# A float32 decoder trunk on one core: position parts ahead of their DMA copies, a fixed order of first loads, and PSUM banks emptied in two rounds

## The chip, the cores and the metric

The kernel runs on 1 core of one Trainium2 chip. The metric is the device time of one execution in microseconds (us); of several runs the median is taken. A stretch of time is given as start:end in us from the start of the span, the time from the first to the last instruction of the profiled execution.

## The reference, cut to what matters

Two layers of a decoder trunk, 512 tokens by 1024 columns, float32 throughout:

```python
def hybrid_layer(x, ...):
    h = rms_norm(x, g_pre)
    proj = h @ w_in                      # 1024 -> 3628 columns, split into four groups of 4 heads x 64
    o_a = dilated_mixture_attention(rope(a_q), rope(a_k), a_v)
    o_b = mla_attention(b_cq, b_ckv, b_kr, ...)       # low-rank q and kv, one rotary key
    o_c = nsa_attention(rope(c_q), ...)               # compressed, selected and window keys
    o_d = stick_breaking_attention(d_q, d_k, d_v)
    mixed = concat(o_a * silu(a_g), o_b * silu(b_g), o_c * silu(c_g), o_d * silu(d_g))
    return x + rms_norm(mixed @ w_out, g_post)
```

For branch C, `compress_blocks` takes 31 overlapping blocks of 32 tokens of a key (and of a value), adds a position embedding to each, and sends each block, flattened to 2048, through two small matrices. The position embedding is what "position parts" means below.

## The kernel before, in words

**Numbers in two parts.** Products are made as three matmuls of two-part numbers: a first part (the value rounded to fp32r) and a remainder (value minus first part). Wherever a result leaves a PSUM bank to be a matmul operand again, ScalarE (ACT) copies the first part out of the bank, and VectorE (DVE) subtracts it from the bank and writes the remainder. Weights come from HBM by DMA into one of four raw buffers; ACT, DVE or GpSimd (POOL) casts the first part, and POOL subtracts (L310, L320).

**The start** (`run`). The x rows (four blocks of 128), the gain `g_pre`, the first part of the constants (with the identity that transposes need) and the first weight chunks are loaded by DMAs from SyncE's queue (SP). TensorE (PE) meanwhile runs WARM matmuls of ones by ones, whose result nobody reads. `norm_t` takes one block of x: square with a sum on ACT (L415), logarithm and exponential on ACT (L397, L398), product with the gain on DVE in two halves (L419), four PE transposes per half into one bank (L424), first part on ACT (L431), remainder on DVE (L432). The first projection matmuls (L456, L457, L459) read 256 columns, so blocks 0 and 1 both, at once. Banks 77 and 78 are the two halves of block 0, banks 79 and 80 those of block 1.

**The projections** (`chunk`, `proj_b`, `proj_d`, `value_out`, `gate`) fill banks on PE; `d_query`, `evac96`, `value_out` and the value part of `proj_b` empty a bank in two pieces: first part of piece 0, remainder of piece 0, first part of piece 1, remainder of piece 1. `block_parts` makes the stationary operands of the block compression: for each of two slots it issues 4 (keys) or 2 (values) DMA copies from SBUF to SBUF that write columns 0 to 495, and then writes the position parts into columns 496 to 511, with a small copy on ACT (L878) and a small subtraction on DVE (L879), both 128x8. PE reads the slots at L905.

**Attention** runs beside the projections: `turn` transposes probabilities (L1105) and empties the bank (L1108 on ACT, L1109 on DVE), `pv` multiplies with the values (L1121), `stick` is branch D with its scans and sums on DVE (L1045 to L1059), `softmax` the others (L1019, L1021, L1029).

**What sets the order.** The program is written by generators that mix attention with projections, and then class `Order` reorders it: it gives each instruction a cost and a latency, builds the graph of what must follow what (`graph`), and simulates the five engines forward and backward, several times. In this graph a bank is one cell: each access to it follows the latest access by every engine, two reads included. A DMA into a slot counts as covering everything between its first and last element. `keep` then fixes the found order on each engine. Engines, and the SP queue, work strictly in that order, so an instruction that waits holds up all that stands behind it on its engine.

Of the kernel before, what the change touches and what calls it, by code (L numbers as in the profile page):

```python
# [172 lines left out]
START = (0, 'c', 1, 'g', 'w', 'w', 'w', 2, 3, 'w')  # L173
PRE = 2
WARM = 32
# [9 lines left out]
class Build:  # L185
# [224 lines left out]
    def norm_t(self, b, x, gpre, h=None):  # L410

        nc = self.nc
        h = h or self.F.get(2)
        ss = self.col()
        nc.scalar.activation(h.ap, x.ap, AF.Square, accum_out=ss)  # L415
        r = self.rstd(ss, D)
        for half in range(2):
            q = slice(512 * half, 512 * half + 512)
            nc.vector.scalar_tensor_tensor(h[:, q], x[:, q], r, gpre[:, q], op0=OP.mult, op1=OP.mult)  # L419
        for half in range(2):  # L420
            t = self.ps(*self.wide)
            for k in range(4):
                kk = half * 4 + k
                nc.tensor.transpose(t[:, k * 128:k * 128 + 128], h[:, kk * 128:kk * 128 + 128], self.ident)  # L424
            tv = t.rearrange("p (k c) -> p k c", k=4)
            pair = [self.nh[j][2 * half:2 * half + 2] for j in range(2)]
            n = 4 if all(q.i == p.i + 2 for p, q in pair) else 2
            for q in range(4 // n):
                hi, lo = (self.R.ap[:, p[q].i * 512:(p[q].i + n) * 512].rearrange("p (k c) -> p k c", k=n)[
                    :, :, b * 128:b * 128 + 128] for p in pair)  # L430
                nc.scalar.copy(hi, tv[:, n * q:n * q + n])  # L431
                nc.vector.tensor_tensor(lo, tv[:, n * q:n * q + n], hi.bitcast(F32), OP.subtract)  # L432
            self.psfree(t)
        h.free()
# [45 lines left out]
    def value_out(self, outs):  # L480

        vs = [self.R.get(2) for _ in range(2)]
        with self.soon():
            for p, out in enumerate(outs):
                ov = out.rearrange("p (b h c) -> p b h c", b=2, h=4)
                for j, v in enumerate(vs):
                    self.value_parts(v.ap.rearrange("p (e b t c) -> p t b e c", e=2, b=4, t=2)[:, :, 2 * p:2 * p + 2],
                                     ov[:, :, 2 * j:2 * j + 2])
                self.psfree(out)
        return vs  # L490
# [87 lines left out]
    def values(self, out):  # L578
# [3 lines left out]
        with self.soon():  # L582
            nc.scalar.copy(v.ap, out)
            self.psfree(out)
            t = self.ps(*self.wide)
            for b in range(NB):
                nc.tensor.transpose(t[:, b * 128:b * 128 + 128], v[:, b * 128:b * 128 + 128], self.ident)
            d = self.R.get(2)
            self.value_parts(d.ap.rearrange("p (e b t c) -> p t b e c", e=2, b=4, t=2),
                             t.rearrange("p (b e c) -> p b e c", b=4, e=2))  # L590
            self.psfree(t)
# [3 lines left out]
    def value_parts(self, d, src):  # L595
        self.nc.scalar.copy(d[:, 0], src)
        self.nc.vector.tensor_tensor(d[:, 1], src, d[:, 0].bitcast(F32), OP.subtract)
# [39 lines left out]
    def proj_b(self, l):  # L637
# [110 lines left out]
        for p in range(2):  # L748
# [4 lines left out]
            with self.soon():  # L753
                ov = out.rearrange("p (b h c) -> p b h c", b=2, h=4)
                for j in range(2):
                    dv = V[j].ap.rearrange("p (h b t c) -> p t b h c", h=2, b=4, t=2)
                    self.value_parts(dv[:, :, 2 * p:2 * p + 2], ov[:, :, 2 * j:2 * j + 2])
# [13 lines left out]
    def evac96(self, out, d):  # L771
        nc = self.nc
        with self.soon():
            for j in range(2):
                s = out[64 * j:64 * j + 64]
                nc.scalar.copy(d[j][0:64, 0], s)
                nc.vector.tensor_tensor(d[j][0:64, 1], s, d[j][0:64, 0].bitcast(F32), OP.subtract)  # L777
        self.psfree(out)

    def d_query(self, p, out):  # L780
        nc = self.nc
        with self.soon():
            for j in range(2):
                s, x = self.R.get(), out[64 * j:64 * j + 64]
                nc.scalar.copy(s[0:64], x)
                nc.vector.tensor_tensor(s[64:128], x, s[0:64].bitcast(F32), OP.subtract)
                self.Dq[2 * p + j] = s
# [77 lines left out]
    def block_parts(self, parts, n, pos):  # L865
# [5 lines left out]
        for i in range(2):  # L871
            d = self.R.get(2)
            for j, s in enumerate(parts):
# [3 lines left out]
            p, q = self.small[:, pos + 8 * i:pos + 8 * i + 8], d.v(2)[:, :, 496:512:2]  # L877
            nc.scalar.copy(q[:, 0], p)  # L878
            nc.vector.tensor_tensor(q[:, 1], p, q[:, 0].bitcast(F32), OP.subtract)  # L879
# [522 lines left out]
    def run(self):  # L1402
# [3 lines left out]
        self.setup()  # L1406
        for step in START:
# [6 lines left out]
            else:  # L1414
                nc.sync.dma_start(xs[step].ap, self.aps["x"][128 * step:128 * step + 128])
        nc.sync.dma_start(self.c[:, C_MA:], c[:, C_MA:])
# [86 lines left out]
class Order:  # L1503
# [6 lines left out]
    def __init__(self, nc, tc):  # L1510
        self.tc = tc
# [95 lines left out]
    def graph(self):  # L1607
# [3 lines left out]
        for k, i in enumerate(self.ins):  # L1611
# [23 lines left out]
            self.after.append(sorted(d))  # L1635
        self.then = [[] for _ in self.ins]
# [22 lines left out]
    def backward(self):  # L1659
# [11 lines left out]
        for _ in range(n):  # L1671
# [7 lines left out]
            for j in self.after[k]:  # L1679
                f = self.eng[j]  # L1680
                busy, lat, _, extra = self.cost[j]
                if f == e == 0:
# [12 lines left out]
    def forward(self, rank):  # L1695
# [13 lines left out]
        for _ in self.ins:  # L1709
# [23 lines left out]
            for j in self.then[k]:  # L1733
                f = self.eng[j]
                ready[j] = max(ready[j], free[e] if f == e == 0 else end[k] + (self.SEES[f] if f != e or e == 4 else 0))
# [16 lines left out]
def build(nc, tc, aps):  # L1752
    with tc.tile_pool(name="sb", bufs=1) as sb, \
# [4 lines left out]
        o = Order(nc, tc)  # L1758
# [46 lines left out]
```

## Time and profile before

| | us |
|---|---|
| median of 3 runs | 662.58 (661.51 to 663.36) |
| the profiled execution | 661.76 |
| its span | 660.0 |
| PE busy in it | 633.2 |
| ACT, DVE, POOL busy | 471.4, 455.5, 384.9 |

The profiled execution took 1.76 us beyond its span and stands 0.82 us under the median. Its page gives the busy time of each engine; the trace gives each instruction's start and duration, and what ended the idle time before it. PE matmuls overlap, so a busy PE is not a PE at its peak. A DVE or POOL instruction's duration includes time in which it has been started but waits for a port of the memory.

### The profile page before, as it was taken

Reading aid. Unit: us, or ns where it says so; the run is one execution under the profiler, and the core shown is the slowest. Engines: PE = TensorE matmul, PEld = TensorE weight load, DVE = VectorE, ACT = ScalarE, POOL = GpSimd, SP = SyncE. Lnnn points to the kernel's source line nnn. Section 1 sums busy time; section 2 is a strip of 40 time slices with the busy share of each in tenths; the row PEclk is TensorE's granted clock in tenths of the full one; section 3 lists DMA queues with packets and bytes.
Section 4 is the critical chain, followed back from the end, with each engine's and each line's share of the span. In section 5 each row is a group of like instructions: output and inputs, shape, how many; then the busy total and the mean of one; then the engine's idle time right before and its main releaser. Section 6 shows DMA issues by size and latency. Waiting matters only on the chain.

```text
span 660.0 us, 10416 instructions
## 1 busy us (share of the span) xinstructions
PE 633.2 (96%) x3488; PEld 531.5 (81%) x3488; DVE 455.5 (69%) x964; ACT 471.4 (71%) x1053; POOL 384.9 (58%) x301
## 2 busy tenths in 40 slices
PE   8999998699999999999999999999999999999996
PEld 8988876588768789877889878877887778987885
DVE  4837999975788666459594875976557956756623
ACT  6276767396989878997434765867987896779911
POOL 3482658467974772986373335195695845666620
PEclk9999999799999999999999999999999999999998
DMA  9465222853453246644444232028546422562121
GB/s 327 153 210 166 77 64 51 202 145 95 124 162 129 65 125 163 189 159 131 141 138 125 81 97 75 1 51 221 159 136 164 149 94 64 137 184 65 65 96 64
DMA packets 36487, 83.25 MB, mean 126 GB/s; under 512 B 7185, under 2 KB 17809, under 8 KB 36433
## 3 DMA queue, kind: packets, MB, share of 16 engines
q1 hardware_dynamic: 36432, 82.59, 42.5%
q8 instruction: 27, 0.44, 0.3%
q14 instruction: 28, 0.22, 0.1%
HBM read 57.66 MB, written 4.19 MB: 94 GB/s over the span
## 4 chain that ended last, share of the span: by engine, by line
PE 65%; ACT 12%; DVE 11%; POOL 3%; issue 3%; DMA 3%; SPq 1%; DVEq 0%; ACTq 0%; POOLq 0%
PE bank L456 9%; PE bank L457 9%; PE bank L459 8%; PE bank L446 6%; PE bank L447 6%; PE bank L448 6%; PE bank L1121 6%; PE bank L1105 5%; ACT arena_f L1021 3%; ACT arena_f L1029 3%; PE bank L974 2%; PE bank L975 2%; DVE arena_f L1057 2%; DVE arena_f L1059 2%; PE bank L905 2%
## 5 line engine op out<-in xcount | busy, mean ns | idle before, releaser
L320 POOL TENSOR_TENSOR arena_r<-raw,arena_r 128x512 fp32r<-128x512 f32 (+1 forms) x150 | 201.6, 1365 | 131.7 <-ACT arena_r L315 91.3
L456 PE MATMUL bank<-arena_r 128*128 128x512 f32 (+1 forms) x416 | 158.9, 387 | 1.0 <-DVE arena_f L725 0.4
L457 PE MATMUL bank<-arena_r 128*128 128x512 f32 (+1 forms) x416 | 157.8, 384 | 0.0
L459 PE MATMUL bank<-arena_r 128*128 128x512 f32 (+1 forms) x416 | 107.4, 380 | 1.1 <-POOL arena_r L320 1.0
L446 PE MATMUL bank<-arena_r 128*128 128x256 f32 (+1 forms) x280 | 96.2, 346 | 0.2 <-DVE arena_r L777 0.2
L1121 PE MATMUL bank<-arena_r 128*128 128x256 f32 (+4 forms) x368 | 85.6, 321 | 10.6 <-DVE arena_r L1109 8.0
L447 PE MATMUL bank<-arena_r 128*128 128x256 f32 (+1 forms) x280 | 95.7, 343 | 0.0
L448 PE MATMUL bank<-arena_r 128*128 128x256 f32 (+1 forms) x280 | 95.0, 342 | 0.0
L1109 DVE TENSOR_TENSOR arena_r<-bank,arena_r 128x512 fp32r<-128x512 f32 (+2 forms) x122 | 71.8, 597 | 29.7 <-ACT arena_r L1108 27.4
L456 PEld LDWEIGHTS bank<-arena_r 128*128 128x128 f32 x416 | 79.8, 192 | 14.2 <-DVE arena_f L725 1.0
L457 PEld LDWEIGHTS bank<-arena_r 128*128 128x128 f32 x416 | 79.7, 192 | 12.1 <-DVE arena_r L432 0.2
L459 PEld LDWEIGHTS bank<-arena_r 128*128 128x128 f32 x416 | 74.2, 189 | 15.6 <-POOL arena_r L320 2.1
L1105 PE MATMUL bank<-consts,arena_f 128*128 128x128 f32 x408 | 79.3, 276 | 1.5 <-DVE arena_r L1109 0.7
L1021 ACT ACTIVATE arena_f<-arena_f,stats 128x512 f32<-128x512 f32 (+3 forms) x128 | 71.1, 557 | 12.3 <-DVE stats L1019 11.6
L1019 DVE CUSTOM_DVE_ANT_0 arena_f<-bank,consts 128x128 f32<-128x128 f32 (+3 forms) x128 | 59.4, 483 | 25.3 <-PE bank L975 14.7
L1121 PEld LDWEIGHTS bank<-arena_r 128*128 128x128 f32 (+1 forms) x368 | 52.8, 163 | 23.7 <-DVE arena_r L1109 9.7
L1108 ACT CAST arena_r<-bank 128x512 fp32r<-128x512 f32 (+2 forms) x122 | 61.5, 512 | 12.9 <-PE bank L1105 10.1
L1029 ACT ACTIVATE arena_f<-arena_f,stats 128x512 f32<-128x512 f32 (+3 forms) x128 | 66.7, 557 | 2.6 <-DVE stats L1028 2.2
L1105 PEld LDWEIGHTS bank<-consts,arena_f 128*128 128x128 f32 x408 | 53.0, 141 | 16.1 <-DVE arena_r L1109 2.5
L315 ACT CAST arena_r<-raw 128x1024 fp32r<-128x1024 f32 (+2 forms) x55 | 56.1, 1024 | 13.1 <-PE bank L457 4.1
L446 PEld LDWEIGHTS bank<-arena_r 128*128 128x128 f32 x280 | 53.1, 190 | 6.7 <-DVE arena_r L777 0.7
L310 POOL TENSOR_TENSOR arena_r<-raw,arena_r 128x512 fp32r<-128x512 f32 x34 | 47.0, 1393 | 18.7 <-ACT arena_r L309 13.3
(159 smaller groups left out, 1175.4 us busy)
## 6 DMA issues: line engine op xcount, KB each, us to landing
raw<-w_in SPq DMA_DIRECT2D x56, 512.0 KB, 3.8
raw<-w_out SPq DMA_DIRECT2D x16, 512.0 KB, 3.4
arena_r<-arena_r SPq DMA_DIRECT2D x56, 128.0 KB, 2.4
arena_r<-arena_r SPq DMA_DIRECT2D x80, 64.0 KB, 2.0
arena_f<-x SPq DMA_DIRECT2D x8, 512.0 KB, 4.1
raw<-w1k SPq DMA_DIRECT2D x8, 512.0 KB, 4.3
raw<-w1v SPq DMA_DIRECT2D x8, 512.0 KB, 3.7
arena_r<-arena_r SPq DMA_DIRECT2D x8, 256.0 KB, 3.2
```

The source lines that it names most:

```text
L320: nc.gpsimd.tensor_tensor(lo[:, q], raw[:, q], h[:, q].bitcast(F32), OP.subtract)
L446: mm(out, wh, xh, start=start, stop=False, skip_group_check=True)
L447: mm(out, wh, xl, start=False, stop=False, skip_group_check=True)
L448: mm(out, wl, xh, start=False, stop=stop, skip_group_check=True)
L456: mm(out[:, q], wh[:, k, :], self.h(0, k)[:, q], start=k == 0, stop=False, skip_group_check=True)
L457: mm(out[:, q], wh[:, k, :], self.h(1, k)[:, q], start=False, stop=False, skip_group_check=True)
L459: mm(out[:, q], wl[:, k - 8, :], self.h(0, k - 8)[:, q], start=False, stop=k == 15, skip_group_check=True)
L1021: nc.scalar.activation(x, x, AF.Exp, bias=nm[:, j:j + 1], scale=-1.0, accum_out=l[:, j:j + 1])
L1029: nc.scalar.activation(parts[j], parts[j], AF.Copy, scale=rj)
L1105: nc.tensor.transpose(t[:, 128 * j:128 * j + 128], b, self.ident)
L1109: nc.vector.tensor_tensor(lo[:, :w], t[:, :w], hi[:, :w].bitcast(F32), OP.subtract)
L1121: mm(o, v, x, start=first and n == 0, stop=last and n == 2 * len(jobs) - 1, skip_group_check=True)
```

## The change

Three edits, and 8 more warm-up matmuls:

- `both` (new) copies the first parts of all pieces of a bank on ACT, and then subtracts all remainders on DVE. `norm_t`, `value_out`, `values`, `evac96`, `d_query` and the value part of `proj_b` go through it (L431 and L432, L596 and L597, L776 and L777, L785 and L786 before; L597 and L599 after).
- `block_parts` writes the position parts of a slot before it issues the slot's DMA copies (L878 and L879 before; L870 and L871 after).
- START, the order of the first loads, becomes x0, gain, constants, x1, two weights, x2, x3, two weights; `Order` now gets the names of these loads and has an edge from each to the next, so that they keep this order on the SP queue. WARM goes from 32 to 40.

```diff
-START = (0, 'c', 1, 'g', 'w', 'w', 'w', 2, 3, 'w')
+START = (0, 'g', 'c', 1, 'w', 'w', 2, 3, 'w', 'w')
-WARM = 32
+WARM = 40
...
-            for j in range(2):
-                s = out[64 * j:64 * j + 64]
-                nc.scalar.copy(d[j][0:64, 0], s)
-                nc.vector.tensor_tensor(d[j][0:64, 1], s, d[j][0:64, 0].bitcast(F32), OP.subtract)
+            self.both([(x[0:64, 0], x[0:64, 1], out[64 * j:64 * j + 64]) for j, x in enumerate(d)])
...
+    def both(self, parts):
+        for hi, _, src in parts:
+            self.nc.scalar.copy(hi, src)
+        for hi, lo, src in parts:
+            self.nc.vector.tensor_tensor(lo, src, hi.bitcast(F32), OP.subtract)
...
             d = self.R.get(2)
+            p, q = self.small[:, pos + 8 * i:pos + 8 * i + 8], d.v(2)[:, :, 496:512:2]
+            nc.scalar.copy(q[:, 0], p)
+            nc.vector.tensor_tensor(q[:, 1], p, q[:, 0].bitcast(F32), OP.subtract)
             for j, s in enumerate(parts):
                 for e in range(2):
                     w = 496 - (i & e)
                     self.dma(d.v(2)[64 * e + n * j:64 * e + n * j + n, :, 0:w], s.v(2)[0:n, :, 16 * i + e:16 * i + e + w])
-            p, q = self.small[:, pos + 8 * i:pos + 8 * i + 8], d.v(2)[:, :, 496:512:2]
-            nc.scalar.copy(q[:, 0], p)
-            nc.vector.tensor_tensor(q[:, 1], p, q[:, 0].bitcast(F32), OP.subtract)
...
+        self.loose = {(at[a], at[b]) for a, b in zip(self.queue, self.queue[1:])}
+        for a, b in self.loose:
+            self.after[b].append(a)
```

Since `Order` plans the whole program anew, instructions move on every engine. Their number and shape stay the same but for the 8 warm-up matmuls. Two places matter below.

**ACT at the start.** L415, L397, L398 are the norm of a block, L315 is the cast of the first weight chunk (raw_65); the casts from banks 77 and 78 (L431 before, L597 after) empty block 0 before, and from 79 and 80 block 1. Before:

```order
L415 ACTIVATE arena_f,stats<-arena_f 128x1024
L397 ACTIVATE stats<-stats 128x1
L398 ACTIVATE stats<-stats 128x1
L415 ACTIVATE arena_f,stats<-arena_f 128x1024
L397 ACTIVATE stats<-stats 128x1
L398 ACTIVATE stats<-stats 128x1
L315 CAST arena_r<-raw_65 128x1024
L431 CAST arena_r<-bank_77 128x4x128
L431 CAST arena_r<-bank_79 128x4x128
L431 CAST arena_r<-bank_78 128x4x128
L431 CAST arena_r<-bank_80 128x4x128
```

After:

```order
L415 ACTIVATE arena_f,stats<-arena_f 128x1024
L397 ACTIVATE stats<-stats 128x1
L398 ACTIVATE stats<-stats 128x1
L597 CAST arena_r<-bank_77 128x4x128
L597 CAST arena_r<-bank_78 128x4x128
L415 ACTIVATE arena_f,stats<-arena_f 128x1024
L397 ACTIVATE stats<-stats 128x1
L315 CAST arena_r<-raw_65 128x1024
L398 ACTIVATE stats<-stats 128x1
L597 CAST arena_r<-bank_79 128x4x128
```

The norm of block 1 (the second L415 to L398) moved from before the first bank to behind the two banks of block 0, and the weight cast moved into it. DVE moved alike: block 1's products (L419) stand behind block 0's two remainders.

**DVE in layer 0, where the queries of branch B leave bank 76.** L1057 and L1059 are a scan and a sum of `stick`, L550 is the last sum of a rotary key (L546 after), L777 (L599 after) the remainder of a query, L1109 (L1105 after) the remainder of transposed probabilities for which PE waits at L1121. Before:

```order
L550 TENSOR_TENSOR arena_f<-arena_f 112x512 [waits DVE_49,Pool_49]
L1057 SCALAR_TENSOR_TENSOR arena_f<-arena_f,consts 128x128 [waits DVE_49]
L1057 SCALAR_TENSOR_TENSOR arena_f<-arena_f,consts 128x384
L777 TENSOR_TENSOR arena_r<-bank_76,arena_r 64x512 [waits Activation_49]
L1059 TENSOR_TENSOR arena_f<-arena_f 128x512 [waits DVE_49]
L1109 TENSOR_TENSOR arena_r<-bank_80,arena_r 128x512
L1109 TENSOR_TENSOR arena_r<-bank_81,arena_r 128x256
L777 TENSOR_TENSOR arena_r<-bank_76,arena_r 64x512 [waits Activation_49]
```

After:

```order
L545 TENSOR_TENSOR arena_f<-arena_f 112x512 [waits Pool_49]
L1053 SCALAR_TENSOR_TENSOR arena_f<-arena_f,consts 128x384
L546 TENSOR_TENSOR arena_f<-arena_f 112x512 [waits DVE_49,Pool_49]
L599 TENSOR_TENSOR arena_r<-bank_76,arena_r 64x512 [waits PE_49,Activation_49]
L871 TENSOR_TENSOR arena_r<-arena_f,arena_r 128x8
L599 TENSOR_TENSOR arena_r<-bank_76,arena_r 64x512
L1055 TENSOR_TENSOR arena_f<-arena_f 128x512 [waits DVE_49]
L871 TENSOR_TENSOR arena_r<-arena_f,arena_r 128x8
L1105 TENSOR_TENSOR arena_r<-bank_80,arena_r 128x512
```

Both remainders of bank 76 and both position subtractions (L871) now stand ahead of the probabilities' remainder; the second L777 stood behind it, and the position subtractions (L879) stood further down, with waits for DMAs that L871 has not here.

## Rows read from the trace of the kernel before

**Rows 1.** Windows: busy us (count) of each engine per stretch, granted PE clock, DMA.

```profile
112.00:124.00 12.00, 4.48 (x18) 3.61 (x17) 11.94 (x9) 3.03 (x7) 7.38 (x6) 0.72 0.75 151
...
430.00:455.00 25.00, 22.47 (x111) 17.42 (x110) 17.18 (x32) 17.02 (x37) 21.00 (x15) 1.00 0.44 89
...
sum 660.00, PE 633.20 PEld 531.54 DVE 455.50 ACT 471.45 POOL 384.94; mean PE 57.56 PEld 48.32 DVE 41.41 ACT 42.86 POOL 34.99
```

**Rows 2.** Waits of PE over the whole span: total us, times, longest.

```profile
PE bank L1121 <- DVE arena_r L1109: 8.0, 2, 7.5
PE bank L905 <- DVE arena_r L879: 2.2, 2, 1.2
```

**Rows 3.** Timeline 0:22: start, duration, engine, line, operation [idle before, releaser].

```profile
1.08 7.09 PE L1419 MATMUL bank<-ones 128*128 128x128 f32 x32 [1.08 <-DVE ones L355]
...
4.19 1.06 ACT L415 ACTIVATE arena_f<-arena_f 128x1024 f32<-128x1024 f32 x1 [2.17 <-DMA arena_f<-x]
...
5.70 0.20 ACT L398 ACTIVATE stats<-stats 128x1 f32<-128x1 f32 x1
...
7.79 2.74 DVE L419 SCALAR_TENSOR_TENSOR arena_f<-arena_f,stats 128x512 f32<-128x512 f32 x4 [6.76 <-DMA arena_f<-g_pre]
...
9.02 1.05 ACT L315 CAST arena_r<-raw 128x1024 fp32r<-128x1024 f32 x1 [1.51 <-DMA raw<-w_in]
...
9.32 3.65 PE L424 MATMUL bank<-consts,arena_f 128*128 128x128 f32 x16 [1.15 <-DVE arena_f L419]
...
10.44 0.59 ACT L431 CAST arena_r<-bank 128x512 fp32r<-128x512 f32 x1 [0.38 <-PE bank L424]
...
12.62 0.56 PE L456 MATMUL bank<-arena_r 128*128 128x256 f32 x1
...
14.47 0.41 PE L456 MATMUL bank<-arena_r 128*128 128x256 f32 x1
...
14.68 0.41 PE L457 MATMUL bank<-arena_r 128*128 128x256 f32 x1
...
15.17 0.28 PE L456 MATMUL bank<-arena_r 128*128 128x256 f32 x1
...
15.29 0.28 PE L457 MATMUL bank<-arena_r 128*128 128x256 f32 x1
```

**Rows 4.** Timeline 107:125, layer 0, columns as in rows 3.

```profile
111.34 3.15 POOL L524 TENSOR_TENSOR arena_r<-arena_f,arena_r 112x512 fp32r<-112x512 f32 x2
...
112.70 7.23 DVE L1059 TENSOR_TENSOR arena_f<-arena_f 128x512 f32<-128x512 f32 x1
...
114.46 3.69 POOL L320 TENSOR_TENSOR arena_r<-raw,arena_r 128x512 fp32r<-128x512 f32 x3
118.12 1.25 POOL L310 TENSOR_TENSOR arena_r<-raw,arena_r 128x512 fp32r<-128x512 f32 x1
...
120.58 0.69 PE L1121 MATMUL bank<-arena_r 128*64 128x128 f32 x2 [7.52 <-DVE arena_r L1109]
...
122.99 0.63 PE L457 MATMUL bank<-arena_r 128*128 128x512 f32 x1
...
124.23 0.40 PE L456 MATMUL bank<-arena_r 128*128 128x512 f32 x1
```

**Rows 5.** Timeline 160:164: POOL and DVE at the same port.

```profile
160.74 3.45 POOL L320 TENSOR_TENSOR arena_r<-raw,arena_r 128x512 fp32r<-128x512 f32 x2
161.37 1.67 DVE L547 TENSOR_TENSOR arena_f<-arena_f,tab 128x512 f32<-128x512 f32 x1
```

**Rows 6.** Timeline 430:455 of PE alone: the same stage in layer 1.

```profile
448.36 0.74 PE L905 MATMUL bank<-arena_r 128*64 128x512 f32 x2 [1.00 <-DVE arena_r L879]
```

**Rows 7.** Timeline 44:49: a bank emptied in two pieces, L785 and L786 alternating.

```profile
44.92 0.58 ACT L785 CAST arena_r<-bank 64x512 fp32r<-64x512 f32 x1 [0.98 <-PE bank L459]
...
46.87 0.69 DVE L786 TENSOR_TENSOR arena_r<-bank,arena_r 64x512 fp32r<-64x512 f32 x1 [0.65 <-ACT arena_r L785]
```

**Rows 8.** Timeline 109:124 of SP: the DMA copies of the stage in rows 4.

```profile
109.43 12.16 SPq L532 DMA_DIRECT2D arena_r<-arena_r  x18
```

## Prediction: how the time is worked out

> **What bounds the kernel now.** I read four views: the totals, the waits of PE, the timeline where PE waits longest, and the start. The totals say PE is the bound: 633.20 us busy in a span of 660.00 [rows 1], so 26.8 us is all that anything but matmuls can give back. The other engines have slack on average; what they cost is paid at single places. PE's waits name two [rows 2]: 8.0 us for a remainder of transposed probabilities (L1121 on L1109, 7.5 of it once), and 2.2 us for a position subtraction (L905 on L879, in two pieces). The rest is the start, the tail and waits under about 1 us.
>
> The long wait is in layer 0 [rows 4]. PE stops until 120.58. DVE was not idle: its sum L1059 lasted from 112.70 to 119.93, 7.23 us, for 512 columns; another DVE operation of 512 columns needs 2.74/4 = 0.69 us [rows 3]. Meanwhile POOL ran six instructions back to back, from 111.34 to 118.12 + 1.25 = 119.37, and the sum ended 0.56 us later, with L1109 queued behind it on DVE. It had been passed over at five starts of a POOL instruction. Elsewhere DVE gets in after one: at 161.37 an operation of DVE comes while POOL works and takes 1.67 us, ending between POOL's pair that runs to 164.19 [rows 5]. So the wait is DVE and POOL meeting at one memory port. It costs more than its idle time: from 120.58 to 124.23 PE's matmuls come slowly, and the stretch 112:124 has a granted clock of 0.72 [rows 1, 4]. Read as 3.65 us at the lower of two levels (1.2 instead of 2.4 GHz), that is half of 3.65, about 1.8 us, lost. Price of the place: 7.5 + 1.8 = 9.3 us.
>
> The Trainium skill, page "SBUF — State Buffer", section "Who interferes with whom", calls this port pair an exclusive lock, held for a whole instruction by whoever issues first. By that the sum would have waited only for the L524 then running (3.15/2 = 1.6 us) and the place would have cost nothing. The trace differs: 7.23 us [rows 4]. The measurement decides.
>
> **The start: +6.0.** Before, 32 warm-up matmuls end at 1.08 + 7.09 = 8.17. The gain, for which DVE waited, is there by 7.79; PE transposes from 9.32, 16 in 3.65 us; a first part on ACT starts at 10.44, 1.12 after the transposes begin, and takes 0.59; the first projection matmul runs at 12.62 [rows 3]. Both blocks' norms on ACT (for one, 4.19 to 5.70 + 0.20, so 1.71 us) were done by then.
>
> After, in the order shown: 8 more warm-up matmuls at 7.09/32 = 0.22 us each end at 9.94. The transposes of bank 77 start there, its copy at 9.94 + 1.12 = 11.06, ending 11.65; bank 78's transposes end at 9.94 + 8 x 0.23 = 11.8, its copy at about 12.55. Only then ACT may do block 1's norm, 1.71, with the weight cast of 1.05 [rows 3] inside it: 15.3. DVE's half product, 0.69: 16.0. Transposes and copy of bank 79, 1.12 + 0.59: the first matmul at 17.7 in place of 12.62, or +5.1. Bank 80's four transposes, 4 x 0.23 = 0.9, lay ahead of the first matmul before and lie behind it in the new order: together +6.0. An earlier gain saves nothing, because PE now waits for the warm-up. On SP's queue x1 moves behind gain and constants; it has until 12.55 to land, and before, the gain, fourth in the list, was there by 7.79. The bounds: PE ran its first projections slowly, 256 columns in 0.21 us from 14.47 to 14.68, against 0.12 from 15.17 to 15.29 [rows 3], which is near 1.2 and 2.4 GHz. If it comes to them at the higher level, about half of 14.9 - 12.62 comes back, 1.1 us: +4.8. If the long wait between the two blocks keeps it low for another stretch like that, 1.1 is added: +7.
>
> **Layer 0's stage: -7.0.** In the new order the subtractions of bank 76, the sum and the position subtractions stand ahead of the probabilities' remainder, and PE has a group of projection matmuls ahead of the L1121 that waits for it. POOL's run (L520, L320, L310) is still there, but at another phase to DVE. Whether DVE is passed over again is the open question; of the two patterns that the trace shows, [rows 5] is the ordinary one. What is left of the wait I take from the same stage of layer 1: in 430:455 PE is busy 22.47 of 25.00 us, so 2.5 us idle [rows 1], of which 1.00 is counted in the next term. I still leave a whole 2.3 in place, since the new order has more DVE work ahead: 9.3 - 2.3 = 7.0. Bounds: 0, if DVE is passed over as before; -9.3, if PE never stops.
>
> **Position parts: -2.2.** L879 wrote into slots still being written by DMAs; PE's two waits for it, 2.2 us in total, 1.00 of them at 448.36 [rows 2, 6], go when L871 needs only ACT's small copy. In exchange the DMA copies now wait on SP's queue until L871 is done, and everything behind them waits too, weight loads included; 18 such issues took 12.16 us [rows 8], so SP is a place where a delay is not caught up quickly. The position work itself is unchanged (four copies and four subtractions of 8 columns). Bounds: -2.2, or up to +2.2 if the copies come as late as the parts did.
>
> **Two rounds per bank: 0.** Alternating, a bank takes from 44.92 to 46.87 + 0.69 = 47.56, 2.64 us; ACT waited 0.75 of that time for DVE and DVE 0.65 for ACT [rows 7]. Two copies of 0.58 and two remainders of 0.69 in a row are 2.54, as the planner's graph orders all accesses of one bank. PE is not released earlier by more than 0.1; against that the first piece's remainder comes one copy, 0.58 us, later. PE has other matmuls meanwhile. Bounds: ±0.5.
>
> **The rest.** All short waits are planned anew, with the same instructions; of the some 7 us outside the places above I keep the sum, 0 ± 3.
>
> **Sum:** +6.0 - 7.0 - 2.2 + 0 = -3.2 on the profiled 661.76: 658.6. That execution is 0.82 under the median, so I predict 659.4 for the median.
>
> **Rivals.** (1) *Slower: POOL keeps the port again.* The run of POOL instructions still stands beside the stage, now with more short DVE subtractions queued behind one sum. If a sum of `stick` (L1055) again starts in the middle of the run, the 7.0 are not gained, and the start is paid: 659.4 + 7.0 = 666.4, or 664 if half is. It decides as soon as DVE is passed over at three POOL starts (some 3.7 us at 3.69/3 each [rows 4]). For it: the mechanism is in the trace at just this place. Against: it takes a meeting within a microsecond. 0.20.
> (2) *Faster: the extra warm-up raises the clock.* If the longer warm-up brings the higher level before the transposes, the 8 extra matmuls cost 0.9 instead of 1.8, the twelve transposes on the path and behind it some 1.3 less, and the slow first projections 1.1 less: the start loses 6.0 - 3.2 = 2.8, and the time is 656.2. Against it: PE was busy from 1.08 to 8.17 and was still slow at 14.68, after a pause of 1.15 us [rows 3]. 0.12. The Trainium skill, "TensorE: Matmul & The Clock Gate", Part 1, says that sustained matmul activity releases the higher clock, and by that rule this rival would be the forecast; the trace shows the clock low after 7 us of activity and agrees only with a late release.
> (3) *SP's queue.* The copies held behind L871 delay PE's L905 and the raw weights behind them by 2 to 4 us in layer 0: 661 to 664. 0.13.
> (4) *The change does not do what it says.* L871 may still wait for DMAs, those of the slot's earlier user; the 2.2 stay: 661.6, and with the re-planned waits 660 to 664. 0.10.
> The forecast's own chance is 0.45, in 656 to 662.
>
> **Range and chances.** A measurement of this kernel can tell 0.3%, 2.0 us, so "same" is 660.6 to 664.6. The range runs from 654 (rival 2 with the better bounds) to 666 (rival 1 but for its end). Faster: three quarters of the forecast (0.34), rival 2 (0.12) and a little of 3 and 4: 0.48. Slower: most of rival 1 and the bad ends of the others: 0.24. Same: 0.28.
>
> **What would show it.** *Start*: ACT copies banks 77 and 78 before block 1's square, and the first projection matmul starts near 17.7; near 13 would make the term wrong. *Stage*: in layer 0 no DVE sum L1055 much over 2 us, and no wait of PE at L1121 over 2; a sum of 5 us and more is rival 1. *Position parts*: PE's waits on L871 near zero, and L871 ahead of the DMAs; a wait of L905 on the DMA copies is rival 3. PE's idle total should come to 26.8 + 6.0 - 5.2 - 2.2, about 25 (1.8 of the stage's gain is clock, not idle time); below 20 or above 32 the sum is wrong.

## The result and the profile after

The changed kernel takes 674.54 us in the median (673.45 to 675.19), against 662.97 of the kernel before beside it: a ratio of 1.0178 (1.0162 to 1.0193), slower by 11.6 us. The forecast was 659.4. The profiled execution took 674.35 us with a span of 672.5. PE is idle for 34.9 us of it, 8.1 more than before, and busy for 637.6, 4.4 more, of which the 8 warm-up matmuls are 8.79 - 7.09 = 1.7; the rest goes with the slower clock shown below and was not measured apart.

The waits of PE in the kernel after (total us, times, longest), against [rows 2]:

```profile
PE bank L453 <- DVE arena_r L599: 5.9, 1, 5.9
PE bank L424 <- DVE arena_f L419: 4.9, 1, 4.9
...
PE bank L1117 <- DVE arena_r L1105: 3.3, 3, 2.0
```

The waits on the position parts (L905 on L879 before, L901 on L871 after) are gone. Two new ones stand ahead of all others: one at the start (L424), one in layer 0 (L453 on L599: the next projection may not write into bank 76 until a query has left it).

To see where time is lost, I summed the columns of all matmuls but the warm-up in order, and read from both traces when the same share of this work is done. How much later the kernel after is there:

| before at | after is later by | place |
|---|---|---|
| 31.9 us | 5.6 us | start |
| 89.7 | 6.2 | |
| 107.3 | 8.9 | layer 0, before the stage |
| 139.4 | 9.2 | behind layer 0's stage |
| 238.4 | 10.4 | layer 0's attention |
| 423.9 | 8.9 | into layer 1 |
| 439.6 | 9.7 | |
| 449.5 | 12.1 | layer 1's stage |
| 649.2 | 12.6 | end |

**The start**, timeline of the kernel after, columns as in [rows 3]:

```profile
1.08 8.79 PE L1417 MATMUL bank<-ones 128*128 128x128 f32 x40 [1.08 <-DVE ones L355]
4.10 1.06 ACT L415 ACTIVATE arena_f<-arena_f 128x1024 f32<-128x1024 f32 x1 [2.09 <-DMA arena_f<-x]
...
11.64 0.59 ACT L597 CAST arena_r<-bank 128x512 fp32r<-128x512 f32 x1 [0.27 <-PE bank L424]
12.12 1.06 ACT L415 ACTIVATE arena_f<-arena_f 128x1024 f32<-128x1024 f32 x1
...
14.67 3.43 DVE L419 SCALAR_TENSOR_TENSOR arena_f<-arena_f,stats 128x512 f32<-128x512 f32 x2 [1.72 <-ACT stats L398]
16.48 1.12 PE L424 MATMUL bank<-consts,arena_f 128*128 128x128 f32 x4 [4.88 <-DVE arena_f L419]
...
18.27 0.58 PE L453 MATMUL bank<-arena_r 128*128 128x256 f32 x1 [0.68 <-ACT arena_r L597]
...
19.72 0.41 PE L453 MATMUL bank<-arena_r 128*128 128x256 f32 x1
19.93 0.41 PE L454 MATMUL bank<-arena_r 128*128 128x256 f32 x1
...
21.45 0.28 PE L454 MATMUL bank<-arena_r 128*128 128x256 f32 x1
21.57 0.28 PE L453 MATMUL bank<-arena_r 128*128 128x256 f32 x1
```

ACT empties both banks of block 0 and only then begins block 1's square, at 12.12. The first projection matmul runs at 18.27 instead of 12.62. The longer warm-up brought no early clock: 256 columns still come 0.21 us apart at 19.72, and 0.12 apart at 21.45.

**Layer 0's stage**, timeline, against [rows 4]:

```profile
119.14 4.22 POOL L520 TENSOR_TENSOR arena_r<-arena_f,arena_r 112x512 fp32r<-112x512 f32 x3
119.66 0.68 DVE L599 TENSOR_TENSOR arena_r<-bank,arena_r 64x512 fp32r<-64x512 f32 x1
120.26 6.79 DVE L871 TENSOR_TENSOR arena_r<-arena_f,arena_r 128x8 fp32r<-128x8 f32 x1
123.33 3.69 POOL L320 TENSOR_TENSOR arena_r<-raw,arena_r 128x512 fp32r<-128x512 f32 x3
126.99 1.25 POOL L310 TENSOR_TENSOR arena_r<-raw,arena_r 128x512 fp32r<-128x512 f32 x1
127.08 0.69 DVE L599 TENSOR_TENSOR arena_r<-bank,arena_r 64x512 fp32r<-64x512 f32 x1
...
127.92 0.77 PE L453 MATMUL bank<-arena_r 128*128 128x512 f32 x1 [5.94 <-DVE arena_r L599]
...
128.72 0.15 DVE L871 TENSOR_TENSOR arena_r<-arena_f,arena_r 128x8 fp32r<-128x8 f32 x1
```

A position subtraction of 8 columns, 0.15 us of work in its second instance, takes 6.79: DVE is passed over at five starts of a POOL instruction, and the second remainder of bank 76, which PE waits for to reuse the bank, is queued behind it.

**Layer 1's stage** has it too, now for DVE's own L520:

```profile
447.79 7.54 DVE L520 TENSOR_TENSOR arena_r<-arena_f,arena_r 128x512 fp32r<-128x512 f32 x1 [0.19 <-ACT arena_r L518]
...
448.53 3.78 POOL L320 TENSOR_TENSOR arena_r<-raw,arena_r 128x512 fp32r<-128x512 f32 x3
452.27 2.50 POOL L310 TENSOR_TENSOR arena_r<-raw,arena_r 128x512 fp32r<-128x512 f32 x2
...
455.71 0.33 PE L1117 MATMUL bank<-arena_r 128*64 128x256 f32 x1 [1.96 <-DVE arena_r L1105]
...
458.36 0.79 PE L443 MATMUL bank<-arena_r 128*128 128x512 f32 x1 [0.91 <-DVE arena_f L561]
```

**The clock** in 12 us windows of the kernel after (columns as in [rows 1]; the granted clock is the third number from the end):

```profile
96.00:108.00 12.00, 10.12 (x40) 7.70 (x39) 11.94 (x19) 7.74 (x15) 1.57 (x1) 0.86 0.14 44
120.00:132.00 12.00, 6.06 (x19) 4.55 (x18) 11.94 (x10) 2.64 (x5) 8.24 (x7) 0.79 0.42 69
132.00:144.00 12.00, 11.83 (x61) 9.63 (x60) 7.93 (x15) 7.36 (x14) 2.53 (x2) 0.93 0.81 208
456.00:468.00 12.00, 10.73 (x54) 8.76 (x54) 8.16 (x20) 10.29 (x23) 5.51 (x5) 0.86 0.94 259
```

Three stretches of waiting are followed by one at the lower level: (0.14 + 0.21 + 0.07 + 0.14) x 12 = 6.7 us lost, some 0.5 of it before PE had work again at 127.92; before, this column shows it at the stage and the tail alone. (At the start the column reads 1.00 in both kernels, though the matmuls come 0.21 us apart there.) The first and the last of the three are new. Near 101 PE waited for ACT twice, and 0.14 x 12 = 1.7 us of clock came on top:

```profile
100.79 0.66 PE L1101 MATMUL bank<-consts,arena_f 128*128 128x128 f32 x4 [1.10 <-ACT arena_f L1056]
...
102.46 0.50 PE L453 MATMUL bank<-arena_r 128*128 128x512 f32 x1 [0.78 <-ACT arena_f L667]
```

The same two waits stand in all twelve traces of the runs below that have the third edit, and in none of the seven without it, the kernel before among them. So they belong to the plans with two rounds. The clock fell behind them in e3 and k1 alone of the twelve, so the 1.7 is not a fixed price.

### The profile page after: what moved, and what is told of

Same layout as the page of the kernel before. It is cut to its first block, busy times and chain, and to the rows that moved or that the text cites. A ratio compares the mean times of both kernels' runs of the same rounds, so it can differ in the third digit from the quotient of the medians.

```text
span 672.5 us, 10441 instructions
## 1 busy us (share of the span) xinstructions
PE 637.6 (95%) x3496; PEld 535.4 (80%) x3496; DVE 465.1 (69%) x964; ACT 471.2 (70%) x1053; POOL 383.1 (57%) x301
## 4 chain that ended last, share of the span: by engine, by line
PE 63%; ACT 16%; DVE 12%; issue 4%; POOL 2%; DMA 1%; SPq 1%; DVEq 0%; ACTq 0%; POOLq 0%
PE bank L453 10%; PE bank L454 10%; PE bank L456 8%; PE bank L445 5%; PE bank L443 5%; PE bank L444 5%; PE bank L1117 4%; PE bank L1101 4%; ACT arena_f L1025 4%; ACT arena_f L1017 3%; ACT arena_r L315 2%; ACT arena_r L1104 2%; PE bank L970 2%; DVE arena_f L1015 2%; DVE arena_r L1105 2%
## 5 line engine op out<-in xcount | busy, mean ns | idle before, releaser
L320 POOL TENSOR_TENSOR arena_r<-raw,arena_r 128x512 fp32r<-128x512 f32 (+1 forms) x150 | 202.1, 1369 | 124.0 <-ACT arena_r L315 85.2
L453 PE MATMUL bank<-arena_r 128*128 128x512 f32 (+1 forms) x416 | 160.5, 391 | 9.0 <-DVE arena_r L599 5.9
L453 PEld LDWEIGHTS bank<-arena_r 128*128 128x128 f32 x416 | 80.6, 194 | 24.2 <-issue 6.5
L1117 PE MATMUL bank<-arena_r 128*128 128x256 f32 (+4 forms) x368 | 87.2, 321 | 6.0 <-DVE arena_r L1105 3.3
L1105 DVE TENSOR_TENSOR arena_r<-bank,arena_r 128x512 fp32r<-128x512 f32 (+2 forms) x122 | 71.9, 598 | 28.1 <-ACT arena_r L1104 27.0
L456 PEld LDWEIGHTS bank<-arena_r 128*128 128x128 f32 x416 | 74.2, 189 | 13.7
L1017 ACT ACTIVATE arena_f<-arena_f,stats 128x128 f32<-128x128 f32 (+3 forms) x128 | 71.2, 558 | 17.2 <-DVE stats L1015 16.8
L1015 DVE CUSTOM_DVE_ANT_0 arena_f<-bank,consts 128x256 f32<-128x256 f32 (+3 forms) x128 | 59.0, 482 | 22.3 <-PE bank L971 17.3
L1025 ACT ACTIVATE arena_f<-arena_f,stats 128x384 f32<-128x384 f32 (+3 forms) x128 | 66.4, 556 | 1.9 <-DVE stats L1024 1.5
L315 ACT CAST arena_r<-raw 128x1024 fp32r<-128x1024 f32 (+2 forms) x55 | 56.0, 1023 | 13.3 <-DMA raw<-w_in 3.4
L310 POOL TENSOR_TENSOR arena_r<-raw,arena_r 128x512 fp32r<-128x512 f32 x34 | 44.5, 1324 | 33.5 <-ACT arena_r L309 20.5
```

Of the source, the lines that this page charges most:

```text
L320: nc.gpsimd.tensor_tensor(lo[:, q], raw[:, q], h[:, q].bitcast(F32), OP.subtract)
L453: mm(out[:, q], wh[:, k, :], self.h(0, k)[:, q], start=k == 0, stop=False, skip_group_check=True)
L456: mm(out[:, q], wl[:, k - 8, :], self.h(0, k - 8)[:, q], start=False, stop=k == 15, skip_group_check=True)
L1017: nc.scalar.activation(x, x, AF.Exp, bias=nm[:, j:j + 1], scale=-1.0, accum_out=l[:, j:j + 1])
L1025: nc.scalar.activation(parts[j], parts[j], AF.Copy, scale=rj)
L1105: nc.vector.tensor_tensor(lo[:, :w], t[:, :w], hi[:, :w].bitcast(F32), OP.subtract)
```

## The experiments

Two causes were suspected: A, the order at the start, and A2, DVE passed over at the port. The rivals: B puts the loss on the other two edits, C on SP's queue, D on the second round of a bank, and E says that DVE waits for something other than the port. Times are medians in us, ratios against the kernel before on the same chip, with a 95% interval.

**One edit at a time**, each planned anew: the hunks of the change, taken alone into the kernel before (the fourth takes the first hunk out of the kernel after).

```diff
e1_loads     + START, its edges in Order, WARM = 40
e2_parts     + block_parts: position parts first
e3_both      + both()
e4_no_loads  + block_parts, + both()
```

> The kernel before with the first edit alone: the new order of first loads, held on SP's queue, and 40 warm-up matmuls. Theory A (this edit carries the late start): the first projection matmul starts near 18.3 us instead of 12.6, and the time is 5 to 6 us above before, about 668.5, give or take 2 for the waits that are planned anew. Rival B (the start is made up later, the loss is made by the other two edits): about 663.

> The kernel before with the second edit alone: position parts ahead of the DMA copies. Theory A: PE's waits on the position parts go, up to 2.2 us, unless DVE is passed over at the port at another place: 660 to 664. Rival C (the copies held behind the position parts on SP's queue delay PE and the weight loads): 666 or more, with waits of PE on DMA copies or on weights.

> The kernel before with the third edit alone: all first parts of a bank, then all remainders. Theory A (costs nothing by itself): 661 to 665, different only where the new plan moves the meeting of DVE and POOL. Rival D (the first piece's remainder comes later and PE waits for it): 666 or more, with new waits of PE on L599.

> The changed kernel without the first edit: old order of loads, 32 warm-up matmuls, the other two edits kept. Theory A (start 5.6, the rest from the port and the new plan): first projection matmul at about 12.6 and about 669 if DVE is still passed over in both layers, 660 to 663 if the new plan happens to avoid it. Rival B (the loss lies in the other two edits): 672 or more.

| run | us | ratio |
|---|---|---|
| e1_loads | 668.48 | 1.0099 (1.0080 to 1.0118) |
| e2_parts | 659.84 | 0.9966 (0.9944 to 0.9987) |
| e3_both | 666.05 | 1.0062 (1.0040 to 1.0085) |
| e4_no_loads | 669.11 | 1.0110 (1.0086 to 1.0133) |

The loads alone cost 5.9, as A said. Without them the changed kernel is at 669.1 (e4), where A has it if DVE is still passed over in both layers, which it is: 6.78 us near 114 and 7.55 near 441. B, that the other two edits make the whole loss, falls; they bring 6.5 of it in this plan. The position parts alone gain 2.8. The two rounds alone lose 3.5, more than A allowed and in D's range, but not as D has it: PE waits 0.2 us on L599 in all; DVE is passed over at two places, L1048 for 5.15 us near 84 and L520 for 7.49 near 443. Every new plan moves the meetings of DVE and POOL: e1 has them at 119 and 446, e2 at 84 alone, the kernel after at 120 and 448. In e2 the wait of rival 3 of the prediction (C here) is real as well, though the time is not C's 666, and the kernel after does not have it:

```profile
126.99 0.47 PE L905 MATMUL bank<-arena_r 128*64 128x512 f32 x1 [2.75 <-DMA arena_r<-arena_r]
```

Since a new plan changes many things at once, the next runs keep the planned order of the changed kernel and change it by hand.

**The start, order kept.** f1 moves on three engines only:

```diff
         o.run()
+        for e, a, to in ((1, (6, 7, 9, 8), 4), (2, (6, 7), 4), (0, (53, 54, 55, 56), 52)):
+            got = [o.order[e][k] for k in a]
+            rest = [k for k in o.order[e] if k not in got]
+            o.order[e] = rest[:to] + got + rest[to:]
         o.keep()
```

> The changed kernel with its planned order kept, but at the start block 1's norm and the weight cast stand ahead of the copies of block 0's banks on ACT, its products ahead on DVE, and bank 80's transposes ahead of the first projection matmul on PE, as before the change. Theory A (the start loses because block 1's norm waits for block 0's banks): first projection matmul at 13 to 13.5 us, time 674.5 - 5 = 669.5. Rival: the time lost at the start is not on the path to the end and comes back as other waits: 672 or more.

668.48, ratio 1.0110 (1.0057 to 1.0164): 6.1 less than the kernel after. The start, timeline of f1:

```profile
8.27 1.06 ACT L415 ACTIVATE arena_f<-arena_f 128x1024 f32<-128x1024 f32 x1 [2.57 <-DMA arena_f<-x]
...
9.68 3.64 PE L424 MATMUL bank<-consts,arena_f 128*128 128x128 f32 x16
...
13.13 0.49 PE L453 MATMUL bank<-arena_r 128*128 128x256 f32 x1
```

A holds: the order on ACT is the loss at the start, and it is not made up later. That it is 13.13 and not 12.62 comes mostly from the warm-up: behind it the sixteen transposes run from 9.68 (9.32 before) without a stop. x1, now fourth on SP's queue, lets ACT begin only at 8.27, but PE does not wait for it here.

**The port: does a gap between POOL's instructions help?** f2 puts 15 memsets of 128x8 into POOL's two runs, f3 the same with f1's start, f4 seven into the kernel before.

```diff
+        for _ in GAPS:
+            nc.gpsimd.memset(gap, 0.0)
...
+        for n, k in reversed(list(enumerate(GAPS))):
+            o.order[3].insert(k, len(o.ins) + n)
```

> The changed kernel with its planned order kept, and between the instructions of POOL's two long runs (layer 0 near 120, layer 1 near 448) a small POOL memset each, 15 in all, which reads nothing from memory. Theory A (DVE is passed over at the port as long as POOL's next reading instruction is ready): DVE gets in at the first memset, no DVE instruction there over 2.2 us, PE's waits at L599 (5.9) and in layer 1 (about 2.5) go and with them the slow clock behind them, time 664 to 667. Rival E (DVE waits for something other than the port, a semaphore or its own operands): the two DVE instructions still take 6.8 and 7.5 us and the time stays within 2 of 674.5.

> Both of the two edits before: the start as before the change and the POOL memsets. Theory A (two separate causes that add): 659 to 662, which is the kernel before less 1 to 4. Rival (they overlap, or a new wait takes their place): 665 or more.

> The kernel before with its planned order kept, and 7 POOL memsets between the instructions of POOL's run in layer 0. Theory A: L1059 takes at most 2.2 us instead of 7.23, PE's wait of 7.5 us goes and the slow clock behind it, time 663 - 7 to 9 = 654 to 656. Rival E: L1059 stays at about 7 us and the time at 663.

| run | us | ratio |
|---|---|---|
| f2_gaps | 673.16 | 1.0188 (1.0135 to 1.0240) |
| f3_norms_gaps | 667.20 | 1.0065 (1.0035 to 1.0095) |
| f4_before_gaps | 656.76 | 0.9930 (0.9907 to 0.9954) |

The theory missed in f2, and in f3 with it, which lands in its rival's range. In f2 DVE's sum (lines are two higher there) is passed over across the memsets, each of which lasts 0.10 us, and in layer 1 L522 takes 7.81:

```profile
122.39 6.26 DVE L1057 TENSOR_TENSOR arena_f<-arena_f 128x512 f32<-128x512 f32 x1
...
122.93 0.10 POOL L1408 MEMSET gap<- 128x8 f32 x1
122.99 1.29 POOL L322 TENSOR_TENSOR arena_r<-raw,arena_r 128x512 fp32r<-128x512 f32 x1
124.23 0.10 POOL L1408 MEMSET gap<- 128x8 f32 x1
124.29 1.29 POOL L322 TENSOR_TENSOR arena_r<-raw,arena_r 128x512 fp32r<-128x512 f32 x1
```

In f4 DVE got in at the first boundary and the sum took 1.24 us, and all ten executions lie between 656.29 and 658.28; the forecast of 654 to 656 is missed by 0.8. So a memset does not secure the port: it went well in one place and not in two others, and which of the two engines gets in was not to be foreseen. Nor did the kernel before lose its turn every time, as it seems: one of its 19 executions beside f1 to f4 took 655.36 us at a granted clock of 0.999, as fast as f4; no trace of it was kept. Rival E is not shown either. The theory was narrowed to A2: POOL's next reading instruction is as ready behind a memset as before, so what has to go is the readiness.

**The port: POOL waits for the DVE instruction.** A real wait on POOL, between two of its own instructions, order kept. TURN pairs a place on POOL with one on DVE.

```diff
+        wait = mybir.DependencyInfo(mybir.DependencyClass.Sync, mybir.DependencyReason.DATA)
+        for p, v in TURN:
+            self.tc.add_manual_dep(self.ins[self.order[3][p]], self.ins[self.order[2][v]].name, wait, reason="turn")
```

> The changed kernel with its planned order kept, and three waits added on POOL, between its own instructions: in layer 0 the second L520 of the run waits for the first L871 on DVE, and the first L320 for the sum L1055; in layer 1 the first L320 after the last L520 waits for DVE's L520. Theory A2 (DVE is passed over because POOL's next instruction is ready; a memset in between leaves it ready, as the run with memsets showed, a wait does not): L871, L1055 and L520 take at most 1.9 us each, PE's 5.9 us at L599 go with most of the slow clock behind it, and about 2.5 us in layer 1: 663 to 667. Rival E (DVE waits for something else): the three stay long, or the program stands, and 674.

> The same three waits and the start of the kernel before (block 1's norm first). Theory A2: the two causes add, 657 to 661, under the kernel before. Rival (they overlap or new waits take their place): 663 or more.

> The kernel before with one wait added: POOL's second L524 of the run in layer 0 waits for DVE's sum L1059. Theory A2: L1059 at most 1.9 us instead of 7.23, 654 to 657. Rival E: 662 to 664.

> The kernel before with the second edit alone (position parts first), and one wait added: near 84 us, where that plan has DVE's L1052 for 5.16 us, POOL's L320 waits for it. Theory A2: L1052 at most 2 us, PE's wait of 3.4 us there goes, 655 to 657. Rival: PE's waits on the DMA copies (3.7 us in that run) set the time, 659 to 660.

| run | us | ratio |
|---|---|---|
| g1_turn | 668.09 | 1.0077 (1.0051 to 1.0102) |
| g2_norms_turn | 663.06 | 1.0008 (0.9990 to 1.0026) |
| g3_before_turn | 656.92 | 0.9914 (0.9891 to 0.9937) |
| g4_parts_turn | 655.57 | 0.9901 (0.9868 to 0.9935) |

In the kernel before one wait is worth 5.8 us. g3's timeline shows the sum at its normal length plus one POOL instruction's rest, and POOL stopping for it (lines one higher):

```profile
113.64 1.14 DVE L1060 TENSOR_TENSOR arena_f<-arena_f 128x512 f32<-128x512 f32 x1
...
114.92 1.28 POOL L525 TENSOR_TENSOR arena_r<-arena_f,arena_r 128x512 fp32r<-128x512 f32 x1 [0.70 <-DVE arena_f L1060]
```

E falls: the DVE instructions waited for POOL's run. That what the two share is the memory port is the prediction's reading; no run here separates it. g1 gains 6.4 and g2 stands level with the kernel before; both miss their ranges, by 1 and 2 us, and g2 lies in its rival's (663 or more). The reason is in g1's rows: the guarded instructions are short, and the next one on DVE without a guard is passed over in their place:

```profile
120.11 0.66 DVE L872 TENSOR_TENSOR arena_r<-arena_f,arena_r 128x8 fp32r<-128x8 f32 x1
...
121.41 1.78 DVE L1056 TENSOR_TENSOR arena_f<-arena_f 128x512 f32<-128x512 f32 x1
123.12 6.14 DVE L872 TENSOR_TENSOR arena_r<-arena_f,arena_r 128x8 fp32r<-128x8 f32 x1
```

In g4 one of the four executions, the profiled one, took 659.19: PE waited 5.7 us for the block's DMA copies in it, and the clock fell twice.

**What is left.** g5 is g2 with that one guarded too, g6 guards three more, g7 guards the two places of e3_both, and h takes the 8 extra warm-up matmuls out of the kernel after.

```diff
-TURN = ((44, 123), (46, 125), (193, 543))
+TURN = ((44, 123), (46, 125), (47, 126), (193, 543))
...
-WARM = 40
+WARM = 32
```

> The run with three waits and the start of before, and a fourth wait: in layer 0 POOL's second L320 of the run waits for the second L871 on DVE. Theory A2 (start and port explain the whole loss): PE's wait of 5.2 us goes and the slow clock behind it, 655 to 658, which is as far under before as the waits bring before itself (656.9). Rival (the other two edits cost something themselves): 660 or more.

> The same and three more waits, where DVE was passed over once (L545 twice for 3.0 and 2.2 us, L871 for 2.4 us). Theory: each costs PE little, 0 to 1.5 us less than the run with four waits. Rival: waits on POOL delay its own work and it becomes slower by 1 or more.

> The kernel before with the third edit alone (two rounds per bank), and two waits on POOL where that plan has DVE passed over: L320 behind L1048 near 84 us, L320 behind DVE's L520 in layer 1. Theory A2 (two rounds cost nothing by themselves): 666 less 5 to 9, 657 to 661. Rival D (the second round delays PE): 664 or more.

> The changed kernel with 32 warm-up matmuls in place of 40, its order the same on every engine otherwise. If the warm-up holds up the first transposes: they start 0.5 to 1.5 us earlier and the time is 673 to 674. If the longer warm-up brings the faster clock: the first projections run slowly for longer and the time is 674.5 or more.

| run | us | ratio |
|---|---|---|
| g5_norms_turn4 | 659.75 | 0.9954 (0.9938 to 0.9970) |
| g6_norms_turn7 | 657.21 | 0.9925 (0.9904 to 0.9946) |
| g7_both_turn | 658.62 | 0.9942 (0.9924 to 0.9960) |
| h_warm32 | 673.33 | 1.0163 (1.0139 to 1.0187) |

g5 comes 1.8 above the range of A2 and just under the rival's; the three short meetings that g6 guards make up 2.5, more than I gave them, and with them the changed kernel, with the start of before, stands level with the kernel before and its one wait (657.2 and 656.9). But these are seven waits against one, so the rival, that the other two edits cost something, is not out. For the third edit it is likely: the two waits near 101 stand in g6 too, and g7 lies 1.7 above g3 in the medians (the intervals of the ratios overlap) and is 2.4 later in the sum of matmul work by 107. With two waits the two rounds are at 658.6, under D's 664, and PE's wait on L599 was 0.2 us in e3: D falls. In h the first transposes start at 7.97 instead of 9.68, but the interval (1.2 us in the medians) overlaps with the kernel after.

The last two: g6 with 32 warm-up matmuls, and g4 with a second wait.

```diff
k1_norms_turn7_warm32  WARM = 32
k2_parts_turn2         TURN = ((34, 87), (101, 293))
```

> The changed kernel with the start of before, seven waits on POOL, and 32 warm-up matmuls. In the changed kernel alone 32 in place of 40 was worth 1.2; here the transposes are no longer held by block 1, so the warm-up is the only thing ahead of them: 0.5 to 1.5 under the run with 40 (657.2), 655.7 to 656.7. If the shorter warm-up leaves the clock low for longer: 657 or more.

> The kernel before with the second edit alone and two waits on POOL (behind L1052 near 84 us, behind L549 near 226 us). If the waits on POOL are all that plan lacked: 654.5 to 656, under the kernel before with its one wait (656.9). If PE's waits on the block's DMA copies set the time: 656 to 658, with 3 us and more of them in the list of waits.

k1 misses: 660.22, 0.9958 (0.9940 to 0.9975). Nothing is gained at the start: PE waits 1.5 us for block 1's product, which hangs on x1. As its rival has it, the slow spacing of 0.21 us lasts longer, until 15.62, where g6 has 0.12 from 14.21; but over all traces with 32 matmuls and the old order on ACT it ends anywhere from 13.7 to 16.4, so one trace does not decide. In its profiled execution, the longest of its runs, 4.6 us more than in g6 go between 458 and 491, with one new wait at 460 for a weight cast whose DMA came late, and the lower clock behind it (0.72 in 456:468):

```profile
459.01 1.04 ACT L316 CAST arena_r<-raw 128x1024 fp32r<-128x1024 f32 x1 [2.08 <-DMA raw<-w_in]
460.11 0.80 PE L454 MATMUL bank<-arena_r 128*128 128x512 f32 x1 [2.30 <-ACT arena_r L316]
```

Why that load comes late there is open. k2 takes 655.50, 0.9895 (0.9867 to 0.9924), 7.3 us under the kernel before and level with g4, so its second wait shows no gain. The rival's waits are there, 4.1 us on the block's DMA copies, but they do not bring the time into its range. k2 beats both kernels, and keeps only the second of the three edits; that it also beats the kernel before with one wait (g3) the intervals do not show.

## Why the prediction was wrong, point by point

- **The start, +6.0**: right. 18.27 - 12.62 = 5.65 at the first matmul, 5.6 in the sum of work, 6.1 by f1. That it fits so closely is in part luck, since two errors in the working offset each other: ACT had block 1's norm done at 14.64, not 15.3, but block 1's two products took 3.43 us beside POOL's L320 (1.41 for block 0's).
- **Layer 0's stage, -7.0**: this step failed. It took "of the two patterns that the trace shows, [rows 5] is the ordinary one" as the forecast. POOL's run, one L520 longer, stood beside more DVE work, and DVE was passed over again, at L871 in place of L1059. The place cost 5.94 of wait and half of 5.9 us at the lower clock (granted 0.50 from 127.92 to about 133.8), 8.9 after 9.3: next to nothing is gained, the lower of the two bounds. Rival 1 had the mechanism, but named L1055 and gave it one place (and half of its 7.0 would have been 662.9, not 664). The cover failed as well: the "group of projection matmuls ahead of the L1121" was itself what waited, for bank 76, whose second remainder the change had put behind L871.
- **Layer 1**: the stage that I took as the measure of what is left (2.5 us idle) got the same stall. PE idle 1.96 + 0.36 + 0.91 and a clock of 0.86 behind it: 2.4 later than before in that stage alone. No term of the sum and no rival held it, nor the 3.3 us gathered by 107 (the waits of 1.10 and 0.78 near 101, and 1.7 of clock), which lie just past the "0 ± 3" of the rest.
- **Position parts, -2.2**: the waits on L879 went as said, and in layer 0 the kernel after makes up some 0.9 there (9.9 to 9.0 in the sum of work), which is lost again by 238 (10.4). In layer 1 the stall took it back. Alone the edit gains 2.8 (e2).
- **Two rounds, 0**: alone +3.5 (e3), with the meetings guarded 658.62 beside g3's 656.92. That any edit re-rolls the port was not in its ± 0.5, nor the two waits near 101 that every plan with this edit has. The sum of a bank, 2.54, holds where ACT's two copies follow each other (45.31 to 47.91 in e3, 2.60); in the kernel after the plan puts other work between them (39.77 to 43.31 and 50.56 to 54.74, 3.5 and 4.2).
- **The clock**: rival 2 did not come (0.21 us apart at 19.72). After a stop of 7.52 before, PE ran slowly for 3.65 us; after one of 5.94 now, for 5.9. One row was not enough to price it. PE's idle total, forecast at about 25, is 34.9, above the 32 that was named as the sign of a wrong sum.

So by parts: 5.6 (start) + 3.3 (from 31.9 to 107.3, 2.7 of it behind 89.7) + 0.3 (stage) + 2.4 (layer 1) + 1.0 (rest) = 12.6, the difference at the end. Start and port are shown by experiment: taking both out of the changed kernel, order otherwise kept, leads from 674.5 to 657.2. Of these 17.3 us, 5.8 are what one wait is worth in the kernel before, which leaves 11.5 of the 11.6. The 3.3 were not tried by themselves, and why the new plan has these waits is open; DVE is busy 11.94 of 12.00 us in 96:108.

## What to carry to other kernels

When a stall comes from two engines meeting at a shared resource, an edit that reorders the program need not remove it, it throws the dice again: keep it in the sum, in every stage where the same run of instructions stands, and do not put it at zero because it is rare. The remedy is to guard the meeting, a wait on the engine that has time, placed before its next instruction in the run, and for each exposed instruction of the other engine. For a first load order, ask what the in-order engine does before the second block, not when the first block is there.

## What the runs showed of the hardware that I had not expected

- A DVE instruction with two operands in SBUF can take as long for 8 columns (6.79 us) as for 512 (7.23), if POOL has instructions ready one behind another. In the kernel before DVE lost at 6 of some 56 such boundaries, in the kernel after at 13 of some 66; neither the time since its start nor the operations tell the two apart in these rows. The Trainium skill's rule (page "SBUF — State Buffer", section "Who interferes with whom"), that the first to issue has the pair for the whole instruction, does not tell who has it next: here a DVE instruction that had been waiting was passed over by up to five that came later.
- POOL memsets between two reading instructions (0.10 us each) do not secure DVE its turn (6.26 and 7.81 us in f2, 1.24 in f4). A semaphore wait on POOL does: the longest guarded instruction took 2.48 us (g5), and POOL stood idle for 0.17 to 0.70 us for it.
- Two waits of 1.10 and 0.78 us, with work between them, were followed by 3.4 us at the lower clock (0.86 in 96:108 of the kernel after) in 3 of the 13 traces that have them; in the other ten the granted clock stayed at 1.00.
